# Four edits to a transformer kernel: table loads, mixers' softmax, token parts, the last expert pair

## The chip, the cores and the metric

The kernel runs on one core of one Trainium2 chip. A core has TensorE (PE, matmuls and transposes), VectorE (DVE), ScalarE (ACT), GpSimd (POOL) and SyncE (SP, which issues the DMAs here); they run at the same time and wait for one another by semaphores. Each engine takes its own instructions strictly in order. The metric is the device time of one execution in microseconds (us). One profiled execution supplies the trace.

## The reference

One sequence of 256 tokens, 1024 wide, all weights float32. Cut to what matters:

```python
for l in range(2):                                     # first block, two layers
    x = x + 0.5 * swiglu_ffn(rms_norm(x, g1[l]), ...)  # width 2816
    h = rms_norm(x, mix_norm[l]); proj = h @ w_in[l]
    y_ret = retention(...)                             # 4 heads of 128, rms_norm, * silu(gate)
    y_mla = mla_attention(...)                         # 8 heads of 64 + 32 rotary, causal
    x = x + concat([y_ret, y_mla]) @ w_o[l]
    x = x + 0.5 * swiglu_ffn(rms_norm(x, g2[l]), ...)
# second block: attention over 8 query and 2 key heads (both directions), a gated
# recurrence in both directions, then routing: the best 2 of 32 experts for each token
s = einsum('bhqd,bhkd->bhqk', qb, kf) * scale          # both attentions
p = softmax(s); o = einsum('bhqk,bhkd->bhqd', p, vf)
```

An expert keeps at most its capacity of tokens; a path for tokens beyond it stands behind a branch on their count.

## The kernel before

The kernel's stages follow one another: feed-forward 1 and mixer 1 and feed-forward 2 of layer 0, the same of layer 1, mixer 2, and the experts (`moe`).

In the dense stages a weight comes from HBM in 1-MB pieces (`loaded`, L319) into a ring of four buffers. `pieces` cuts each 128x1024 part into a high half `wh` on ACT (L332) and a remainder `wl` on DVE (L342). A product is the sum of high by high, high by low and low by high: L360 and L363 in the feed-forward, L284 to L286 in the mixers. L380 adds the bank sums of a feed-forward step, and L509 and L513 make the gated product. SP issues a load when its buffer is free.

`load_small` is a generator that the first feed-forward calls once per step from step HOOK_AT on. Its steps load the constant tables (L164), the gain columns (L175), the gain rows (L195), and the router weights (L203, L204). The last step also multiplies these by a gain on POOL (L207) and calls `rotary`, which loads the positions (L235) and works out sine and cosine tables on DVE.

In mixer 1, `mla` transposes queries and keys (`heads_T`, L612), and `scores` of a head pair computes score banks `s0` and `s1`, their maxima (L688, L689), the negative scaled maximum (L690), four exponentials on ACT (L693), reciprocals (L695), and the product with these, on DVE (L696) and on POOL (L697). PE then transposes the probabilities (L123, `pb`). The `retention` generator runs interleaved with it; its output `y` is multiplied by the gate on DVE (L807) and transposed.

In mixer 2, `attention` transposes queries and keys (`xa`; `kx` is the key pair with halves swapped, L899), copies them to `qT` (L897) and `kE` (L903, L904), and has one loop of nine turns: scores of (head pair, token half) in each of eight turns, and the transposes of the turn before. L916 to L923 are its softmax. The gated recurrence's work (L976 to L1112) and the big product interleave with it.

The order on each engine is the tile framework's: a scheduler with a simulated timeline sets it when the kernel is built, from the code's dependences, the interleaving of the generators, and the buffers of each tile.

In `moe`, L1329 and L1330 split the tokens into a rounded part `hk[0]` and a remainder `hk[1]`. L1381 to L1387 give each token its slot, L1495 and L1496 make the factors `gg` by which PE gathers tokens for four experts (L1508). Experts run in 16 pairs: gate and up (L1527), the hidden values (L1548), their transposes (L123), down (L1574) and the scatter back (L1599). Weights stream through 18 buffers of 1 MB; `blocks` sets the order of the loads, and the main loop at the end of `moe` sets that of the compute. The last pair's down weights come in smaller pieces (`LAST`).

Of the kernel before, what the change touches and what calls it, by code (L numbers as in the profile page):

```python
# [19 lines left out]
S = 256  # L20
DFF = 2816
EPS = 1e-6
P = 128
# [15 lines left out]
HOOK_AT = 3  # L39
# [58 lines left out]
def emit(ctx, tc, A, out):  # L98
# [61 lines left out]
    def load_small():  # L160
        cst = []
# [43 lines left out]
        late.update(cst=cst, gcol=gcol, rw=rw, gperm=gperm)  # L205

        nc.gpsimd.tensor_tensor(rw, rw, gains("g_ffn_2", 0)[:, :, None].to_broadcast([P, 8, 40]), op=ALU.mult)  # L207
        rotary()
# [25 lines left out]
    def rotary():  # L234
        nc.sync.dma_start(posi, A["positions"].rearrange("o (t p) -> p (o t)", p=P))  # L235
        with tc.tile_pool(name="rp", bufs=1) as rp:
# [315 lines left out]
    def mixer1(l):  # L552
        w_in, w_o = A["w_in"][l], A["w_o"][l]
        xp, rs = norm_parts(gains("mix_norm", 8 * l)), norm()
        with tc.tile_pool(name="mx", bufs=2) as m:
            yp = [None, pair_tile(m, [P, 4, S], "y1", bufs=1)]
            gtab = {}
            for nm in ("qn_rope", "kn_rope"):
# [7 lines left out]
                gtab[nm] = (tcos, tsin)  # L566
            cmask = m.tile([P, P], BF16, name="cmask", bufs=1)
# [39 lines left out]
            def heads_T(dst, src, t, gname):  # L607
                for h0 in (0, 4):
                    ps = aux_bank().rearrange("p (a t) -> p a t", a=4)
                    for h in range(4):  # L610
                        flip(ps[:96, h], src[:, h0 + h], ident)
                    nc.scalar.activation(dst[:96, h0:h0 + 4, t * P:(t + 1) * P], ps[:96], AF.Copy,  # L612
                                         scale=gains(gname, l, 1)[:96])

            def mla():
# [53 lines left out]
                scale = 96.0 ** -0.5  # L669
                po = None  # L670
                def scores(hp):
# [16 lines left out]
                    nc.vector.tensor_reduce(mx[:, 0:2], s0, axis=AX.X, op=ALU.max)  # L688
                    nc.vector.tensor_reduce(mx[:, 2:4], s1, axis=AX.X, op=ALU.max)  # L689
                    nc.vector.tensor_scalar(mx[:, 0:4], mx[:, 0:4], -scale, None, op0=ALU.mult)  # L690
                    for i, (dst, src) in enumerate(((p0[:, 0], s0[:, 0]), (p0[:, 1], s0[:, 1]), (p1[:, 0], s1[:, 0]),
                                                    (p1[:, 1], s1[:, 1]))):
                        nc.scalar.activation(dst, src, AF.Exp, bias=mx[:, i:i + 1], scale=scale,  # L693
                                             accum_out=mx[:, 4 + i:5 + i])
# [69 lines left out]
            def retention():  # L764
# [40 lines left out]
                for t in range(2):  # L805
                    y = ys[t]
                    nc.vector.tensor_tensor(y, rg[:, t], y, op=ALU.mult)  # L807
# [16 lines left out]
    def mixer2():  # L824
# [3 lines left out]
        with tc.tile_pool(name="m2l", bufs=1) as ml:  # L828
# [33 lines left out]
            def attention():  # L862
                for nm in ("q_norm_2", "k_norm_2"):
# [7 lines left out]
                    tab[nm] = (tcos, tsin)  # L871
                qT = late4("qT", [P, 4, S])
                kE = late4("kE", [P, 2, 2, S])
                nc.gpsimd.memset(kE, 0.0)
                for t in range(2):
# [21 lines left out]
                    nc.scalar.activation(qT[:, :, ts], ps, AF.Copy)  # L897
                    kx = m.tile([P, 2, 64], F32, tag="kx", name="kx", bufs=1)
                    nc.vector.tensor_copy(kx, x[:, 8:10][:, ::-1])  # L899
                    ps = aux_bank().rearrange("p (a t) -> p a t", a=4)  # L900
                    flip(ps[:, 0], x[:, 8:10].rearrange("p h d -> p (h d)"), ident)
                    flip(ps[:, 1], kx.rearrange("p h d -> p (h d)"), ident)
                    nc.vector.tensor_copy(kE[0:64, :, 0, ts], ps[0:64, 0:2])  # L903
                    nc.vector.tensor_copy(kE[64:128, :, 1, ts], ps[64:128, 0:2][:, ::-1])  # L904
                    yield
                asc = 64.0 ** -0.5
                po = None

                def scores(hp, t):
# [5 lines left out]
                    mx = m.tile([P, 4], F32, tag="mx", name="mx")  # L915
                    nc.vector.tensor_reduce(mx[:, 0:2], ps, axis=AX.X, op=ALU.max)  # L916
                    nc.vector.tensor_scalar(mx[:, 0:2], mx[:, 0:2], -asc, None, op0=ALU.mult)
                    pb = m.tile([P, 2, S], F32, tag="pb", name="pb")
                    for j in range(2):
                        nc.scalar.activation(pb[:, j], ps[:, j], AF.Exp, bias=mx[:, j:j + 1], scale=asc,  # L920
                                             accum_out=mx[:, 2 + j:3 + j])
# [819 lines left out]
```

## Time and profile before

| | |
|---|---|
| runs | 1708.24, 1712.7, 1713.85 us (median 1712.7) |
| profiled execution | 1712.65 us, span 1710.9 us, mean granted clock 0.99 |
| PE busy | 1647.1 us (96%) |
| DVE busy | 1004.8 us (59%) |
| ACT busy | 711.2 us (42%) |
| POOL busy | 361.4 us (21%) |
| DMA | 407.77 MB, mean 238 GB/s |

The first feed-forward fills the time to about 120 us, the mixers of layers 0 and 1 stand around 250 to 310 and 720 to 830 us, the second mixer's attention around 1045 to 1130, and the experts go from 1235 to the end. A share of busy time is a mean over stages with different limits: in the dense stages PE has the work, in the experts the weights' stream does. So waits and windows are to be read stage by stage. In a window's row the columns are busy microseconds, with the number of instructions in brackets; PEclk is TensorE's granted clock, as a share of the full 2.4 GHz, in which 0.5 is the lower level of 1.2 GHz.

### The profile page before, as it was taken

To read this page: it belongs to the slowest core of one execution; us is meant where nothing else is said; L and a number is where in the kernel's file an instruction comes from. 1 tells how busy PE (TensorE), PEld (TensorE's weight loads), DVE (VectorE), ACT (ScalarE), POOL (GpSimd) and SP (SyncE) were. 2 spreads that over 40 slices of the span, in tenths; PEclk is the share of its full clock that TensorE was granted. 3 is DMA by queue.
4 is the path that set the end of the run, shared out by engine and by line. 5 is a ranking of instruction groups with operands and counts; after the bars stand their busy time and mean duration, and the time that the engine had idled before them with its cause. 6 is when DMAs were issued, how large, how long until landed. Compare 5 with 4: busy or idle time off the path is not lost.

```text
span 1710.9 us, 23281 instructions
## 1 busy us (share of the span) xinstructions
PE 1647.1 (96%) x9169; PEld 1234.4 (72%) x9169; DVE 1004.8 (59%) x1571; ACT 711.2 (42%) x1097; POOL 361.4 (21%) x308
## 2 busy tenths in 40 slices
PE   8999998999999999999999999899899999999997
PEld 6788887888888888877888889789744444434332
DVE  6796687876667676787876668976742222211111
ACT  5554466465545554565555446644300000000001
POOL 6333322332222222311422230430400000000000
PEclk9999999999999999999999999999999999999999
DMA  9556552565556555533565565334979999999996
GB/s 315 168 176 200 163 172 75 170 186 186 180 190 195 177 188 174 174 124 122 174 190 174 184 195 168 124 100 150 418 293 404 420 419 421 419 420 421 419 421 263
DMA packets 216598, 407.77 MB, mean 238 GB/s; under 512 B 10063, under 2 KB 177190, under 8 KB 192166
## 3 DMA queue, kind: packets, MB, share of 16 engines
q1 hardware_dynamic: 216486, 406.25, 66.2%
q8 instruction: 74, 1.21, 0.3%
q14 instruction: 38, 0.31, 0.1%
HBM read 405.17 MB, written 1.05 MB: 237 GB/s over the span
## 4 chain that ended last, share of the span: by engine, by line
PE 76%; DMA 11%; DVE 6%; POOL 3%; issue 2%; ACT 1%; SPq 1%; POOLq 0%; DVEq 0%; ACTq 0%
PE mm L360 28%; PE mm L363 14%; PE aux L1527 8%; DMA raw<-in_w_exp_down_dram 6%; PE aux L1574 4%; PE mm L284 4%; PE mm L285 4%; PE mm L286 4%; DMA raw<-in_w_exp_gate_dram 2%; DMA raw<-in_w_exp_up_dram 2%; DVE wl L342 2%; PE aux L1508 2%; PE mm L1599 1%; PE aux L123 1%; ACT wh L332 1%
## 5 line engine op out<-in xcount | busy, mean ns | idle before, releaser
L342 DVE TENSOR_TENSOR wl<-raw,wh 128x1024 fp32r<-128x1024 f32 (+4 forms) x392 | 504.4, 1288 | 207.6 <-ACT wh L332 205.4
L332 ACT ACTIVATE wh<-raw 128x1024 fp32r<-128x1024 f32 (+3 forms) x392 | 405.7, 1037 | 364.0 <-PE mm L360 202.4
L360 PE MATMUL mm<-x,wh 128*128 128x512 f32 x1456 | 483.6, 398 | 10.6 <-DVE gu L380 5.3
L363 PE MATMUL mm<-x,wl 128*128 128x256 f32 x1456 | 361.8, 282 | 0.0
L360 PEld LDWEIGHTS mm<-x,wh 128*128 128x128 f32 x1456 | 271.4, 189 | 74.9 <-DVE gu L380 6.2
L363 PEld LDWEIGHTS mm<-x,wl 128*128 128x128 f32 x1456 | 256.2, 189 | 4.2
L1527 PE MATMUL aux<-raw,xg 128*64 128x512 f32 x1024 | 242.3, 598 | 7.8 <-DMA raw<-in_w_exp_up_dram 7.8
L360 PE MATMUL mm<-h,wh 128*128 128x512 f32 x704 | 246.6, 393 | 0.0
L509 POOL TENSOR_TENSOR gu<-gu,rb 128x512 f32<-128x512 f32 x88 | 141.9, 1616 | 322.9 <-DVE gu L380 299.8
L363 PE MATMUL mm<-h,wl 128*128 128x256 f32 x704 | 196.6, 279 | 0.0
L1527 PEld LDWEIGHTS aux<-raw,xg 128*64 128x64 f32 x1024 | 74.9, 137 | 148.4 <-issue 130.1
L360 PEld LDWEIGHTS mm<-h,wh 128*128 128x128 f32 x704 | 131.9, 187 | 31.6
L1574 PE MATMUL aux<-raw,hd 128*64 128x512 f32 x512 | 136.0, 597 | 4.6 <-DMA raw<-in_w_exp_down_dram 4.6
L363 PEld LDWEIGHTS mm<-h,wl 128*128 128x128 f32 x704 | 131.9, 187 | 0.0
L383 ACT ACTIVATE yp<-aux 128x512 fp32r<-128x512 f32 x32 | 19.1, 597 | 243.8 <-PE aux L1574 243.8
L1574 PEld LDWEIGHTS aux<-raw,hd 128*64 128x64 f32 x512 | 44.8, 136 | 84.2 <-issue 67.2
L1548 DVE SCALAR_TENSOR_TENSOR hid<-aux,cols,g 128x512 f32<-128x512 f32 x16 | 18.0, 1124 | 141.4 <-PE aux L1527 141.4
L384 DVE TENSOR_TENSOR yp<-aux,yp 128x512 fp32r<-128x512 f32 x32 | 22.1, 691 | 109.6 <-ACT yp L383 109.6
L285 PE MATMUL mm<-wl,x 128*128 128x512 f32 (+2 forms) x208 | 78.9, 382 | 0.8 <-DVE wl L342 0.8
L284 PE MATMUL mm<-wh,x 128*128 128x512 f32 (+2 forms) x208 | 77.1, 384 | 1.3 <-ACT wh L332 1.3
L286 PE MATMUL mm<-wh,x 128*128 128x512 f32 (+2 forms) x208 | 78.3, 380 | 0.0
L284 PE MATMUL mm<-x,wh 128*128 128x256 f32 x272 | 78.2, 287 | 0.0
(404 smaller groups left out, 2187.8 us busy)
## 6 DMA issues: line engine op xcount, KB each, us to landing
raw<-in_w_exp_gate_dram SPq DMA_DIRECT2D x64, 1024.0 KB
raw<-in_w_exp_up_dram SPq DMA_DIRECT2D x64, 1024.0 KB
raw<-in_w_exp_down_dram SPq DMA_DIRECT2D x62, 1024.0 KB
raw<-in_ffn_w_up_dram SPq DMA_DIRECT2D x44, 1024.0 KB
raw<-in_ffn_w_gate_dram SPq DMA_DIRECT2D x43, 1024.0 KB
raw<-in_w_in_dram SPq DMA_DIRECT2D x36, 1024.0 KB
raw<-in_ffn_w_down_dram SPq DMA_DIRECT2D x32, 1024.0 KB
raw<-in_ffn_w_down_dram SPq DMA_DIRECT2D x16, 768.0 KB
```

What stands on the lines that cost most here:

```text
L284: nc.tensor.matmul(ps, a[0], b[0], start=first, stop=False, skip_group_check=True)
L285: nc.tensor.matmul(ps, a[0], b[1], start=False, stop=False, skip_group_check=True)
L286: nc.tensor.matmul(ps, a[1], b[0], start=False, stop=last, skip_group_check=True)
L332: nc.scalar.activation(h, r[:, k0:k1], AF.Copy)
L342: eng.tensor_tensor(lf, rf, hf.bitcast(F32), op=ALU.subtract)
L360: nc.tensor.matmul(banks[j], lhs, chunk_both(xp, kk), start=kk == 0, stop=False, skip_group_check=True)
L363: nc.tensor.matmul(banks[j][:, :S], lhs, chunk(xp, kk)[0], start=False, stop=kk == k_all - 1, skip_group_check=True)
L384: nc.vector.tensor_tensor(dst[1][sl], src, dst[0][sl].bitcast(F32), op=ALU.subtract)
L509: nc.gpsimd.tensor_tensor(e, e, twice(rb), op=ALU.mult)
L1508: nc.tensor.matmul(ps[:, i], src[:, t, (k0 + i) * P:(k0 + i + 1) * P], gs[t][:, q0:q0 + n], start=(i, j, t) == terms[0], stop=(i, j, t) == ...
L1527: nc.tensor.matmul(ps[half(s)], xg[:, k, at + s * SLOT:at + (s + 1) * SLOT], w[s][:, k % 4], start=k == 0, stop=k == 7, skip_group_check=True)
L1574: nc.tensor.matmul(pss[hf][half(s)], hd[:, ff, half(s)], w[s][:, ff - ks.start, hf * 512 - c0:(hf + 1) * 512 - c0], start=ff == 0, stop=ff ...
```

## The change

Four edits.

1. The hook starts at step 2 of the first feed-forward in place of 3. The positions are loaded first in it. `rotary` is a generator now: its work is spread over three more steps.
2. In mixer 1 the score factor goes into the query gain column (`gqs`), the reduces return the negated maximum, and L690 is gone. The gate products of both halves of `y` stand ahead of a yield.
3. In mixer 2 the factor goes into the copy `qT`, L917 is gone likewise, `kx` and `kE` are copied by ACT, and the probabilities are transposed two turns behind their scores, with three buffers of `mx` and `pb`.
4. In `moe` the remainder `hk[1]` is taken on DVE, and for the last pair the down weights of the pair before are loaded, and multiplied, ahead of its own up weights.

```diff
-HOOK_AT = 3
+HOOK_AT = 2
@@ load_small
+        nc.sync.dma_start(posi, A["positions"].rearrange("o (t p) -> p (o t)", p=P))
         cst = []
...
         late.update(cst=cst, gcol=gcol, rw=rw, gperm=gperm)
+        yield
         nc.gpsimd.tensor_tensor(rw, rw, gains("g_ffn_2", 0)[:, :, None].to_broadcast([P, 8, 40]), op=ALU.mult)
-        rotary()
+        yield from rotary()
@@ rotary
-        nc.sync.dma_start(posi, A["positions"].rearrange("o (t p) -> p (o t)", p=P))
...
             nc.vector.scalar_tensor_tensor(n1, nh, -4096.0, n1, op0=ALU.mult, op1=ALU.add)
+            yield
             for c in parts:
...
             for i, (shift, add) in enumerate(((0.25, math.pi / 2), (0.0, 0.0))):
+                yield
                 whole(n1, ang, 1 / (2 * math.pi), shift)
@@ mixer1
+            gcols = {"qn_nope": m.tile([P, 1], F32, name="gqs", bufs=1), "kn_nope": gains("kn_nope", l, 1)}
+            nc.vector.tensor_scalar(gcols["qn_nope"], gains("qn_nope", l, 1), 96.0 ** -0.5, None, op0=ALU.mult)
...
-                                         scale=gains(gname, l, 1)[:96])
+                                         scale=gcols[gname][:96])
...
-                    nc.vector.tensor_reduce(mx[:, 0:2], s0, axis=AX.X, op=ALU.max)
-                    nc.vector.tensor_reduce(mx[:, 2:4], s1, axis=AX.X, op=ALU.max)
-                    nc.vector.tensor_scalar(mx[:, 0:4], mx[:, 0:4], -scale, None, op0=ALU.mult)
+                    nc.vector.tensor_reduce(mx[:, 0:2], s0, axis=AX.X, op=ALU.max, negate=True)
+                    nc.vector.tensor_reduce(mx[:, 2:4], s1, axis=AX.X, op=ALU.max, negate=True)
...
-                        nc.scalar.activation(dst, src, AF.Exp, bias=mx[:, i:i + 1], scale=scale,
-                                             accum_out=mx[:, 4 + i:5 + i])
+                        nc.scalar.activation(dst, src, AF.Exp, bias=mx[:, i:i + 1], accum_out=mx[:, 4 + i:5 + i])
...
                 for t in range(2):
+                    nc.vector.tensor_tensor(ys[t], rg[:, t], ys[t], op=ALU.mult)
+                yield
+                for t in range(2):
                     y = ys[t]
-                    nc.vector.tensor_tensor(y, rg[:, t], y, op=ALU.mult)
@@ mixer2
-                    nc.scalar.activation(qT[:, :, ts], ps, AF.Copy)
-                    kx = m.tile([P, 2, 64], F32, tag="kx", name="kx", bufs=1)
-                    nc.vector.tensor_copy(kx, x[:, 8:10][:, ::-1])
+                    nc.scalar.activation(qT[:, :, ts], ps, AF.Copy, scale=asc)
+                    kx = m.tile([P, 2 * S], F32, tag="osq", name="kx", bufs=1)[:, :P]
+                    nc.scalar.activation(kx.rearrange("p (h d) -> p h d", h=2), x[:, 8:10][:, ::-1], AF.Copy)
...
-                    nc.vector.tensor_copy(kE[0:64, :, 0, ts], ps[0:64, 0:2])
-                    nc.vector.tensor_copy(kE[64:128, :, 1, ts], ps[64:128, 0:2][:, ::-1])
+                    nc.scalar.activation(kE[0:64, :, 0, ts], ps[0:64, 0:2], AF.Copy)
+                    nc.scalar.activation(kE[64:128, :, 1, ts], ps[64:128, 0:2][:, ::-1], AF.Copy)
...
-                    mx = m.tile([P, 4], F32, tag="mx", name="mx")
-                    nc.vector.tensor_reduce(mx[:, 0:2], ps, axis=AX.X, op=ALU.max)
-                    nc.vector.tensor_scalar(mx[:, 0:2], mx[:, 0:2], -asc, None, op0=ALU.mult)
-                    pb = m.tile([P, 2, S], F32, tag="pb", name="pb")
+                    mx = m.tile([P, 4], F32, tag="mx", name="mx", bufs=3)
+                    nc.vector.tensor_reduce(mx[:, 0:2], ps, axis=AX.X, op=ALU.max, negate=True)
+                    pb = m.tile([P, 2, S], F32, tag="pb", name="pb", bufs=3)
...
-                pT, last = None, None
-                for i in range(9):
+                pT, pbs = None, []
+                for i in range(10):
                     if i < 8:
-                        pb = scores(i // 2, i % 2)
-                    if last is not None:
-                        hp, t = (i - 1) // 2, (i - 1) % 2
+                        pbs.append(scores(i // 2, i % 2))
+                    if i > 1:
+                        last = pbs[i - 2]
+                        hp, t = (i - 2) // 2, (i - 2) % 2
@@ moe
-                    nc.gpsimd.tensor_tensor(hk[1][:, t], xs[:, t], hk[0][:, t].bitcast(F32), op=ALU.subtract)
+                    nc.vector.tensor_tensor(hk[1][:, t], xs[:, t], hk[0][:, t].bitcast(F32), op=ALU.subtract)
...
+                            if w is wg_ and p == NP - 1:
+                                yield from downs(p - 1)
...
-                    elif p:
-                        for fh in range(2):
-                            for e in (2 * p - 2, 2 * p - 1):
-                                yield by_rows(wd_[e], 4)[:, 2 * fh:2 * fh + 2], 2
+                    elif 0 < p < NP - 1:
+                        yield from downs(p - 1)
...
+                if p == NP - 1:
+                    ys[p - 1] = down(p - 1)
                 if p < NP:
                     run(up(p))
                     run(coming)
-                if p:
+                if p and p != NP - 1:
                     ys[p - 1] = down(p - 1)
```

`downs(p)` yields the four 1-MB down pieces of a pair. Lines of the changed file stand 1 to 11 further down than the same lines before.

What this does to the order. SP in the first feed-forward, where the hook's loads stand among the weights; before, the last of them:

```order
L195 DMA brow_846<-in_b_router_expert_dram 128x32
L319 DMA raw<-in_ffn_w_gate_dram 128x8x256
L319 DMA raw<-in_ffn_w_up_dram 128x8x256
L202 DMA gperm<-in_g_ffn_dram 128x8
L203 DMA rw<-in_w_router_group_dram 128x8x4
L204 DMA rw<-in_w_router_expert_dram 128x8x32
L235 DMA posi<-in_positions_dram 128x2x1
L319 DMA raw<-in_ffn_w_gate_dram 128x8x256
L319 DMA raw<-in_ffn_w_up_dram 128x8x256
```

and now, the first of them:

```order
L322 DMA raw<-in_ffn_w_gate_dram 128x8x256
L322 DMA raw<-in_ffn_w_up_dram 128x8x256
L161 DMA posi<-in_positions_dram 128x2x1
L165 DMA cst_510<-in_cst_dram 128x1744
L165 DMA cst_512<-in_cst_dram 128x1536
L165 DMA cst_514<-in_cst_dram 128x448
L322 DMA raw<-in_ffn_w_gate_dram 128x8x256
L322 DMA raw<-in_ffn_w_up_dram 128x8x256
```

The positions come before the constant tables, and both ahead of the fourth pair of weight loads instead of the fifth; the three router loads (L203 to L205 now) keep their order and stand one pair of weights earlier too.

PE in the second mixer, from the first scores (`kE,qT`) to the second transposes of probabilities (`pb`); the rows left out are L284 to L286 of the big product. Before:

```order
L913 MATMUL aux<-kE,qT 128x256 x4
L284 MATMUL mm<-x_9399,wh 128x256
...
L286 MATMUL mm<-x_9399,wl 128x256
L123 MATMUL aux<-ident,pb 128x128 x4
L1074 MATMUL aux<-qp,kp 128x128 x8
L913 MATMUL aux<-kE,qT 128x256 x2
L123 MATMUL aux<-ident,pb 128x128 x4
L1074 MATMUL aux<-qp,kb 128x128 x8
L945 MATMUL mm<-pT,xa 64x256 x4
```

and now:

```order
L287 MATMUL mm<-x_9394,wh 128x256
L918 MATMUL aux<-kE,qT 128x256 x2
L288 MATMUL mm<-x_9394,wh 128x256
...
L918 MATMUL aux<-kE,qT 128x256 x2
L1078 MATMUL aux<-qp,kp 128x128 x8
L287 MATMUL mm<-x_9395,wh 128x256
...
L289 MATMUL mm<-x_9395,wl 128x256
L918 MATMUL aux<-kE,qT 128x256 x2
L287 MATMUL mm<-x_9394,wh 128x256
...
L288 MATMUL mm<-x_9394,wh 128x256
L123 MATMUL aux<-ident,pb 128x128 x4
L1078 MATMUL aux<-qp,kb 128x128 x8
L289 MATMUL mm<-x_9394,wl 128x256
```

Three sets of scores and the product `qp,kp` stand ahead of the first transposes, where two sets stood, and 43 rows lie between the first scores and these transposes in place of 21.

DVE at the same place, with the softmax (reduce, reciprocal, product) among weight remainders. Before:

```order
L342 TENSOR_TENSOR wl<-raw,wh 128x1024
L976 SCALAR_TENSOR_TENSOR hgs<-th,hgs 128x512
L916 TENSOR_REDUCE mx<-aux 128x2 x2
L1026 TENSOR_SCALAR hgs<-hgs,gcol 128x512
L917 TENSOR_SCALAR mx<-mx 128x2 x2
L1024 TENSOR_TENSOR hgs<-mm,rb 128x512
L342 TENSOR_TENSOR wl<-raw,wh 128x1024
L922 RECIPROCAL mx<-mx 128x2
L923 TENSOR_TENSOR pb<-pb,mx 128x512
L922 RECIPROCAL mx<-mx 128x2
L923 TENSOR_TENSOR pb<-pb,mx 128x512
```

and now:

```order
L345 TENSOR_TENSOR wl<-raw,wh 128x1024
L921 TENSOR_REDUCE mx<-aux 128x2 x2
L345 TENSOR_TENSOR wl<-raw,wh 128x1024
L1081 COPY_PREDICATED A<-cst_512,aux 128x4x128
L926 RECIPROCAL mx<-mx 128x2
L1081 COPY_PREDICATED A<-cst_512,aux 128x4x128
L926 RECIPROCAL mx<-mx 128x2
L927 TENSOR_TENSOR pb<-pb,mx 128x512 x2
L1028 TENSOR_TENSOR hgs<-mm,rb 128x512
L921 TENSOR_REDUCE mx<-aux 128x2
L345 TENSOR_TENSOR wl<-raw,wh 128x1024
```

The scaling of the maximum is gone, one weight remainder and two masked copies of `A` stand between the reduces and the products, and `hgs` is worked on later.

PE at the end of the program, the last two pairs of experts. Before:

```order
L1599 MATMUL mm<-yp,gt 128x512 x2
L1527 MATMUL aux<-raw,xg 64x512 x31
L1574 MATMUL aux<-raw,hd 64x512 x2
L123 MATMUL aux<-ident,hid 128x128 x4
L1574 MATMUL aux<-raw,hd 64x512 x14
L1599 MATMUL mm<-yp,gt 128x512 x6
L1574 MATMUL aux<-raw,hd 64x512 x2
L1599 MATMUL mm<-yp,gt 128x512 x2
L1574 MATMUL aux<-raw,hd 64x512 x13
L1599 MATMUL mm<-yp,gt 128x512 x2
L1574 MATMUL aux<-raw,hd 64x512
L1599 MATMUL mm<-yp,gt 128x512 x6
```

and now:

```order
L1608 MATMUL mm<-yp,gt 128x512 x2
L1536 MATMUL aux<-raw,xg 64x512 x15
L1583 MATMUL aux<-raw,hd 64x512 x16
L1608 MATMUL mm<-yp,gt 128x512 x6
L1536 MATMUL aux<-raw,xg 64x512
L1608 MATMUL mm<-yp,gt 128x512 x2
L1536 MATMUL aux<-raw,xg 64x512 x15
L123 MATMUL aux<-ident,hid 128x128 x4
L1583 MATMUL aux<-raw,hd 64x512 x16
L1608 MATMUL mm<-yp,gt 128x512 x8
```

Sixteen rows of down (`raw,hd`) of pair 14 and its scatter stand ahead of the last up, and all sixteen of pair 15 stand in one piece ahead of the last eight of the scatter.

## Rows read from the trace of the kernel before

**Rows 1.** The page: the chain of waits by engine; GB/s in 40 slices
```profile
PE 76%; DMA 11%; DVE 6%; POOL 3%; issue 2%; ACT 1%; SPq 1%; POOLq 0%; DVEq 0%; ACTq 0%
GB/s 315 168 176 200 163 172 75 170 186 186 180 190 195 177 188 174 174 124 122 174 190 174 184 195 168 124 100 150 418 293 404 420 419 421 419 420 421 419 421 263
```
**Rows 2.** Waits of PE: line, releaser, total us, times, longest
```profile
PE aux L1527 <- DMA raw<-in_w_exp_up_dram: 7.8, 8, 1.3
PE aux L1508 <- DVE gg L1496: 6.3, 1, 6.3
PE aux L123 <- DVE mx L922: 6.1, 2, 4.4
...
PE aux L123 <- DVE pb L696: 1.8, 1, 1.8
PE aux L123 <- DVE y L807: 1.5, 1, 1.5
PE aux L123 <- DVE kx L899: 1.5, 1, 1.5
```
**Rows 3.** Windows: us, busy PE, PEld, DVE, ACT, POOL, PEclk, DMA share, GB/s
```profile
80.00:85.00 5.00, 5.00 (x17) 4.26 (x16) 5.00 (x9) 1.86 (x4) 1.11 (x1) 0.52 0.65 210
...
290.00:295.00 5.00, 2.48 (x17) 1.88 (x18) 4.86 (x8) 2.68 (x8) 1.19 (x1) 0.80 0.35 110
295.00:300.00 5.00, 5.00 (x20) 4.04 (x20) 2.09 (x5) 1.24 (x3) 0.00 (x0) 0.52 0.00 0
...
785.00:790.00 5.00, 5.00 (x28) 3.54 (x28) 4.22 (x8) 2.99 (x6) 1.21 (x1) 0.71 0.00 0
...
1095.00:1100.00 5.00, 5.00 (x29) 4.78 (x28) 3.25 (x7) 1.88 (x3) 0.00 (x0) 0.66 0.60 201
...
1240.00:1245.00 5.00, 1.35 (x6) 1.38 (x7) 4.24 (x8) 0.00 (x0) 2.48 (x2) 0.50 1.00 415
1245.00:1250.00 5.00, 5.00 (x21) 2.93 (x20) 0.85 (x2) 0.00 (x0) 0.00 (x0) 0.63 0.06 26
```
**Rows 4.** Timeline at 76 to 80: start, us, engine, line, instruction, idle before
```profile
76.62 0.17 DVE L238 CAST pos<-posi 128x2 f32<-128x2 int32 x1 [5.62 <-DMA posi<-in_positions_dram]
...
79.49 3.78 PE L360 MATMUL mm<-x,wh 128*128 128x512 f32 x8 [3.78 <-DVE gu L380]
```
**Rows 5.** Timeline of DVE and ACT in mixer 1 of layer 1
```profile
775.67 0.42 DVE L688 TENSOR_REDUCE mx<-aux 128x2 f32<-128x256 f32 x1 [0.21 <-PE aux L681]
...
779.04 1.28 ACT L693 ACT_TABLE_LOAD   x1 [3.15 <-DVE mx L690]
```
**Rows 6.** Timeline of DVE in mixer 2
```profile
1089.90 1.28 DVE L916 TENSOR_REDUCE mx<-aux 128x2 f32<-128x512 f32 x2
```
**Rows 7.** Timeline of POOL and DVE in the routing; the page's group of L342
```profile
1237.84 4.64 POOL L1330 TENSOR_TENSOR hk<-xs,hk 128x1024 fp32r<-128x1024 f32 x2 [4.91 <-ACT hk L1329]
...
1238.06 2.15 DVE L1381 TENSOR_SCALAR over<-rank 128x4 f32<-128x4 f32 x1
1240.12 0.15 DVE L1382 SCALAR_TENSOR_TENSOR slot<-idx,rank 128x4 f32<-128x4 uint32 x1
1240.31 2.19 DVE L1383 SCALAR_TENSOR_TENSOR slot<-over,slot 128x4 f32<-128x4 f32 x1
...
1257.98 0.29 DVE L1416 TENSOR_SCALAR at<-cst,rank 128x128 f32<-128x128 f32 x1 [1.07 <-PE aux L1420]
...
L342 DVE TENSOR_TENSOR wl<-raw,wh 128x1024 fp32r<-128x1024 f32 (+4 forms) x392 | 504.4, 1288 | 207.6 <-ACT wh L332 205.4
```
**Rows 8.** Timeline of PE and DVE in the last two pairs
```profile
1674.99 3.22 PE L1527 MATMUL aux<-raw,xg 128*64 128x512 f32 x13 [1.32 <-DMA raw<-in_w_exp_up_dram]
...
1678.75 1.09 DVE L1548 SCALAR_TENSOR_TENSOR hid<-aux,cols,g 128x512 f32<-128x512 f32 x1 [15.81 <-PE aux L1527]
...
1692.67 6.22 PE L1574 MATMUL aux<-raw,hd 128*64 128x512 f32 x26
...
1703.12 0.73 PE L1599 MATMUL mm<-yp,gt 128*128 128x512 f32 x2 [0.39 <-DVE yp L384]
```

More of the change, by code (lines that the diff above doesn't have):

```diff
@@ L667, in mla @@
                     yield
-                scale = 96.0 ** -0.5
                 po = None
@@ L871, in attention @@
                     tab[nm] = (tcos, tsin)
+                asc = 64.0 ** -0.5
                 qT = late4("qT", [P, 4, S])
@@ L896, in attention @@
                         flip(ps[:, a], x[:, 2 * a:2 * a + 2].rearrange("p h d -> p (h d)"), ident)
-                    nc.scalar.activation(qT[:, :, ts], ps, AF.Copy)
-                    kx = m.tile([P, 2, 64], F32, tag="kx", name="kx", bufs=1)
-                    nc.vector.tensor_copy(kx, x[:, 8:10][:, ::-1])
+                    nc.scalar.activation(qT[:, :, ts], ps, AF.Copy, scale=asc)
+                    kx = m.tile([P, 2 * S], F32, tag="osq", name="kx", bufs=1)[:, :P]
+                    nc.scalar.activation(kx.rearrange("p (h d) -> p h d", h=2), x[:, 8:10][:, ::-1], AF.Copy)
                     ps = aux_bank().rearrange("p (a t) -> p a t", a=4)
                     flip(ps[:, 0], x[:, 8:10].rearrange("p h d -> p (h d)"), ident)
-                    flip(ps[:, 1], kx.rearrange("p h d -> p (h d)"), ident)
-                    nc.vector.tensor_copy(kE[0:64, :, 0, ts], ps[0:64, 0:2])
-                    nc.vector.tensor_copy(kE[64:128, :, 1, ts], ps[64:128, 0:2][:, ::-1])
+                    flip(ps[:, 1], kx, ident)
+                    nc.scalar.activation(kE[0:64, :, 0, ts], ps[0:64, 0:2], AF.Copy)
+                    nc.scalar.activation(kE[64:128, :, 1, ts], ps[64:128, 0:2][:, ::-1], AF.Copy)
                     yield
-                asc = 64.0 ** -0.5
                 po = None
@@ L914, in scores @@
                                          skip_group_check=True)
-                    mx = m.tile([P, 4], F32, tag="mx", name="mx")
-                    nc.vector.tensor_reduce(mx[:, 0:2], ps, axis=AX.X, op=ALU.max)
-                    nc.vector.tensor_scalar(mx[:, 0:2], mx[:, 0:2], -asc, None, op0=ALU.mult)
-                    pb = m.tile([P, 2, S], F32, tag="pb", name="pb")
+                    mx = m.tile([P, 4], F32, tag="mx", name="mx", bufs=3)
+                    nc.vector.tensor_reduce(mx[:, 0:2], ps, axis=AX.X, op=ALU.max, negate=True)
+                    pb = m.tile([P, 2, S], F32, tag="pb", name="pb", bufs=3)
                     for j in range(2):
-                        nc.scalar.activation(pb[:, j], ps[:, j], AF.Exp, bias=mx[:, j:j + 1], scale=asc,
+                        nc.scalar.activation(pb[:, j], ps[:, j], AF.Exp, bias=mx[:, j:j + 1],
                                              accum_out=mx[:, 2 + j:3 + j])
@@ L949, in attention @@
                                 split(ap_, (slice(None), slice(hp - 1, hp + 1)), po)
-                    last = pb if i < 8 else None
                     yield
@@ L1447, in blocks, with downs @@
             def blocks():
+                def downs(p):
+                    for fh in range(2):
+                        for e in (2 * p, 2 * p + 1):
+                            yield by_rows(wd_[e], 4)[:, 2 * fh:2 * fh + 2], 2
                 for p in range(NP + 1):
```

## The prediction

> **What bounds the kernel now.** The chain of waits comes first: it runs through TensorE (PE) for 76% of the span and through DMA for 11% [rows 1]. So a saving on another engine counts only where PE stands still or is throttled. The table of PE's waits is read next. Its long single entries are the ones that the change touches: 6.3 us for the gather factors L1496, 4.4 us in one piece for the softmax sums L922 of the second mixer, and 1.5 to 1.8 us each for L696, L807 and L899 [rows 2]. The largest entry of all, the experts' up weights, is 1.3 us at the most in one piece and is not touched. Then the windows: the reader is to look for a small PE busy time and, in the same or the next window, a granted clock under 1.00 [rows 3]. A stall is paid twice here. PE idles, and what follows runs at half its level (0.52 is nearly all at 1.2 GHz). I count the second part as PE's busy time in the window times one minus its clock. Last, the rate of DMA over the span: from the experts' first loads on it stays at 418 to 421 GB/s, with a dip to 293 [rows 1] that holds the window 1245:1250 (26 GB/s) [rows 3], where loads wait for buffers that PE has not read yet. So the experts' stream resumes when PE resumes, and I pass every microsecond won before it on to the end.
>
> **Small loads and rotary tables.** The cast of the positions stands on VectorE (DVE) behind their DMA, which SP issues behind the router weights; DVE idles 5.62 us for it, and L380, queued behind it, comes late: PE waits 3.78 us [rows 4]. The window 80:85 has PE full at 0.52, so 2.4 us more: 6.2 us in all [rows 3]. In the new order the positions load first of all in the hook, and the table is spread over three more steps. That wait must go. What can come late in its place is L380 behind one weight remainder (L342, 1.29 us, rows 7) and some table operations, since the same DVE work has to go somewhere. I take 4.5, with 0 and 6.2 as ends. The price on SP: positions and three constant tables (1.9 MB) now stand one weight pair earlier. I cost this at nothing because those weights have a PE step ahead of them; without that cover it is the fourth rival.
>
> **First mixer, twice.** Scale and sign go into the queries and the reduce, so each head pair loses L690, and its first exponentials wait for the first reduce alone. In layer 1 that reduce starts at 775.67 and lasts 0.42, but the exponentials' table load starts at 779.04, released by L690 [rows 5]. It can now start at about 776.1, 2.9 us earlier; the second pair of exponentials still needs L689. PE's 1.8 us wait for L696 [rows 2] and the 1.4 us at clock 0.71 [rows 3] come to 3.2. I take 3, ends 0 and 4.5 (a wait for POOL's half of the probabilities goes too, unseen in these rows). In layer 0 the products L807 of both halves stand one yield earlier, so their 1.5 us goes [rows 2]; windows 290:295 and 295:300 hold 2.52 idle and 2.4 lost to the clock [rows 3], 4.9 in all. PE also waits there for copies that do not change, so I take 2, ends 0 and 4.9.
>
> **Second mixer.** Scores of a head pair are now two steps ahead of their transposes: a third copy of two tiles. DVE loses eight 128x2 instructions at about 0.15 (nearest: L1382, rows 7), two key copies and four half-height copies. ScalarE gains the six copies; it is busy for 1.88 of 5 us in the window 1095:1100 [rows 3], so there is room, but not in a certain place. What PE waits 4.4 us for is a reduce that starts at 1089.90 [rows 6] because DVE is full, then exponentials and a product. In the new order 43 rows of PE lie between the first scores and their transposes in place of 21, and on DVE one weight remainder and two masked copies between reduce and product. PE idle 4.4 and 1.5, with 1.7 lost at 0.66 [rows 2, 3] plus the second wait for L922 (6.1 less 4.4 is 1.7): 9.3 if all goes. DVE carries the same weight work in the same stretch, so two thirds can come back as other waits, and moving PE's instructions ahead can add one wait as long as the one removed. Ends -3 and 9.3; I take 3, nearer to the waits whose cause is removed outright (1.5 and 1.7) than to the sum.
>
> **Routing.** POOL's two subtractions L1330 take 4.64 us. Beside them DVE's L1381 takes 2.15 and L1383 2.19, while L1382, of the same 128x4, takes 0.15 [rows 7]. They are the path to L1496, for which PE waits 6.3. With the subtractions on DVE, which orders them behind the gather factors, 4.0 us goes. They cost DVE two times 1.29 (L342, two inputs, same size), ahead of the combine weights that L1420 multiplies; DVE stands idle for 1.07 us there, waiting for PE [rows 7], so 1.5 of the 2.6 is late: 2.5. If the shorter gap also spares the clock (0.50 and 0.63 in two windows, 0.7 and 1.9 us, rows 3), 5.1. Ends -1.5 and 5.1, I take 2.5. The Trainium skill, page "SBUF — State Buffer", section "Who interferes with whom", says that a VectorE instruction with two SBUF inputs, or in its two-port mode, and a GpSimd instruction share one port pair, and the later of them is blocked for the whole of the other. By that rule the 4.0 are POOL's and go; without it only the coincidence of these rows speaks for it, the term would be -1.5, and the sum 4.0 less. It also says that the moved subtractions could block or be blocked by POOL in their new place; POOL is at 0.00 in the window 1245:1250 [rows 3], so the trace of before shows it nothing to meet there.
>
> **Last pair.** Down of pair 14 goes ahead of up of pair 15. Up's second half now waits for 4 MB more: 1674.99 [rows 8] plus 10.0 at 419 GB/s, 1685.0. The path from there to down 15 is hid (3.76 us after it, 1.09 long, rows 8), transposes and a copy, 6.3 in all: 1691.3. Then 32 matmuls at 0.24 (26 in 6.22) end at 1698.9, and the last scatter starts 1.8 later, as before, or when the other scatters queued behind are through, at 1701.2 against 1703.12 [rows 8]. I take 2, ends -1 and 3.
>
> **Sum.** 4.5 + 3 + 2 + 3 + 2.5 + 2 = 17.0 us off the profiled execution's own 1712.65 us (span 1710.9, the rest around it), which equals the median of the runs, 1712.7. That gives 1696.
>
> **Rivals.**
> 1. Waits move. DVE stays the engine that PE waits for, and only the two waits go that have an outside cause: the positions' DMA (3.78) and POOL's neighbours (2.5): 1706. For it: DVE is above 4 of 5 us busy in four of the seven windows of rows 3. Against: four of six terms shorten chains, not only loads.
> 2. The experts' stream hides routing and last pair: 4.5 less, 1700. For it: 419 GB/s to the end. Against: 26 GB/s in 1245:1250.
> 3. All the ends at once, the clock held too: 6.2 + 4.5 + 4.9 + 6 + 5.1 + 2 = 29, 1684. Against: full DVE windows.
> 4. Slower: ScalarE becomes late in the second mixer. It takes the six copies and, with scores at other places among the gates, its function tables may be switched back and forth around the exponentials, 1.28 us a load [rows 5], 2.6 a switch and return. Over eight steps that is 20.5 us on the path. With the other terms won (14.0) it ends at 1719, and it decides from six switched steps on. Against: the exponentials stand among the gates without loads now. The hook's loads are the smaller case of this kind: 4.6 us of transfer (1.9 MB at 419 GB/s), not enough alone.
> 5. It does not relieve what it moves: the order's new places make other waits as long, 1712.
>
> **How the numbers follow.** My forecast 0.47, rival 1 0.22, rival 2 0.08, rival 3 0.08, rival 4 0.07, rival 5 0.08. About 0.3%, 5 us, can be told from no change, so faster means under 1707.6. Rival 1 falls there in three of four cases: faster 0.47 + 0.08 + 0.08 + 0.16 = 0.79; same 0.06 + 0.08 = 0.14; slower 0.07. The forecast's own range is 1690 to 1702 (a third of the terms' spread each way). The range for 8 in 10 reaches from 1686 to 1709: it takes in rivals 1 and 2 and leaves out 3, 4 and 5.
>
> **What would show it.** Right: no idle time of DVE behind the positions, and no window under 1.00 at 75 to 85; the exponentials' table load of layer 1 right behind L688; L1381 and L1383 (L1385 and L1387 after) at 0.2; the wait for L1496 at some 2 us; the second mixer's wait for L922 under 2; scatter last at about 1.9 us sooner against up's arrival. Wrong: DVE waits of the same length under another name in the same windows (rival 1), table loads between the exponentials of the second mixer and PE waiting for ScalarE (rival 4), or a span of the experts that grows by what the dense part loses (rival 2).

## The result

The changed kernel takes 1694.5 us (median of 4 runs, 1692.9 to 1695.7), the kernel before 1712.1 in the runs beside it. The ratio is 0.9900 with a 95% interval of 0.9884 to 0.9916, that is 14 to 20 us less. Forecast were 1696, and 17.0 less. The sum held; its terms did not, as the stages show.

The page after: the chain by engine, and the rate of DMA, as in [rows 1].

```profile
PE 69%; DMA 19%; DVE 6%; ACT 2%; issue 2%; POOL 1%; SPq 0%; ACTq 0%; DVEq 0%; POOLq 0%
GB/s 294 199 174 200 169 164 85 150 198 177 185 188 190 183 184 182 179 140 86 199 186 188 181 193 176 125 124 147 420 321 405 420 420 420 420 421 420 420 421 294
```

PE's waits after (line, releaser, total, times, longest). Of those in [rows 2], L922 and L899 are gone, and L1505 (L1496 before) is at 2.5 for 6.3. New are many short waits for L383 (L380 before) and one of 2.8 for y.

```profile
PE mm L363 <- DVE gu L383: 5.9, 6, 1.5
...
PE aux L123 <- DVE y L809: 3.1, 2, 2.8
...
PE aux L1517 <- DVE gg L1505: 2.5, 2, 2.3
...
PE aux L123 <- DVE pb L699: 1.1, 1, 1.1
```

To place the time, I take the start of the same PE instruction in both timelines at each stage's border (the norm's L430 ahead of the next stage, L1137, L1370, the first L1574, the end of the last scatter L1599; L360's end for the first feed-forward). What its lead over the kernel before grows by within a stage is that stage's gain. The table has it for the changed kernel's trace, and for those of the five kernels below that hold one edit alone; positive is gained, in us; bold is the stage that the edit changes. The stretches between these stages are left out.

| stage | forecast | after | hook_alone | mix1_alone | mix2_alone | hk_alone | last_alone |
|---|---|---|---|---|---|---|---|
| first feed-forward (32 to 205) | 4.5 | 1.0 | **2.0** | -0.3 | 0.3 | 0.1 | 0.0 |
| mixer 1, layer 0 (214 to 338) | 2 | -1.0 | 0.2 | **-2.7** | 2.8 | 2.8 | 1.1 |
| mixer 1, layer 1 (710 to 834) | 3 | 4.1 | 0.7 | **4.2** | 0.8 | 0.0 | -1.2 |
| mixer 2 (1020 to 1154) | 3 | 9.3 | -1.5 | -0.5 | **9.3** | -0.5 | -0.6 |
| routing (1237 to 1290) | 2.5 | 3.5 | -0.2 | -0.1 | 0.2 | **3.0** | 0.3 |
| experts (1290 to the last scatter) | 2 | 2.9 | 0.0 | -0.5 | 0.2 | -0.1 | **1.2** |

The columns show also what one execution can move without any edit: 0.2 to 2.8 us in layer 0's mixer, whose code is the same in four of the five, and 1.8 the other way in layer0_old below.

### The profile page after: what moved, and what is told of

It is laid out like the page before. It is cut to its first block, busy times and chain, and to the rows that moved or that the text cites. A ratio compares the mean times of both kernels' runs of the same rounds, so it can differ in the third digit from the quotient of the medians.

```text
span 1691.1 us, 23257 instructions
## 1 busy us (share of the span) xinstructions
PE 1637.6 (97%) x9169; PEld 1230.0 (73%) x9169; DVE 997.1 (59%) x1553; ACT 712.6 (42%) x1103; POOL 359.2 (21%) x306
## 4 chain that ended last, share of the span: by engine, by line
PE 69%; DMA 19%; DVE 6%; ACT 2%; issue 2%; POOL 1%; SPq 0%; ACTq 0%; DVEq 0%; POOLq 0%
PE mm L363 29%; PE mm L366 15%; DMA raw<-in_w_exp_down_dram 8%; DMA raw<-in_w_exp_gate_dram 6%; DMA raw<-in_w_exp_up_dram 5%; PE mm L287 4%; PE mm L288 4%; PE mm L289 4%; PE aux L1536 4%; DVE wl L345 2%; PE aux L1583 2%; PE aux L123 1%; PE aux L1517 1%; ACT wh L335 1%; PE mm L1608 1%
## 5 line engine op out<-in xcount | busy, mean ns | idle before, releaser
L335 ACT ACTIVATE wh<-raw 128x1024 fp32r<-128x1024 f32 (+3 forms) x392 | 405.2, 1036 | 364.6 <-PE mm L363 199.3
L512 POOL TENSOR_TENSOR gu<-gu,rb 128x512 f32<-128x512 f32 x88 | 142.3, 1620 | 321.6 <-DVE gu L383 298.6
L287 PE MATMUL mm<-wh,x 128*128 128x512 f32 (+2 forms) x208 | 77.2, 384 | 1.3 <-ACT wh L335 1.3
L382 ACT ACTIVATE gu<-mm 128x256 f32<-128x256 f32 x176 | 63.4, 374 | 34.9 <-PE mm L366 34.9
```

The costliest lines, as they stand in the source:

```text
L287: nc.tensor.matmul(ps, a[0], b[0], start=first, stop=False, skip_group_check=True)
L335: nc.scalar.activation(h, r[:, k0:k1], AF.Copy)
L382: nc.scalar.activation(dst[:, j], b[:, S:], AF.Copy)
L512: nc.gpsimd.tensor_tensor(e, e, twice(rb), op=ALU.mult)
```

## The experiments

All are timed in 5 rounds beside the kernel before. The first five hold one edit each, on the kernel before (hk_alone and last_alone hold half of edit 4 each).

**hook_alone**, edit 1 alone. 

> The kernel before with edit 1 alone (hook from step 2, positions first, tables spread over steps). Theory A, the parts are worth what the shift of PE between the stages of the two traces says: 1.0 us faster than before; DVE never waits for the positions, PE waits for L380 some five times for 0.3 to 1.4 us between 65 and 115, no window there under clock 1.00. Theory B, the forecast's term: 4.5 us faster, at most one such wait. Theory C, the parts depend on one another: neither.

Measured: 1708.3 us, ratio 0.9986 (0.9973 to 0.9998), 0.3 to 4.6 us less. Theory A's 1.0 lies inside that, the term of 4.5 at its edge. In its own trace the waits for L380's counterpart are five, 3.4 us in all, and the stage gains 2.0. Its window from 65 to 115 (columns as in rows 3):

```profile
65.00:115.00 50.00, 46.64 (x260) 39.77 (x259) 45.63 (x86) 25.14 (x42) 15.34 (x10) 1.00 0.62 191
```

The same window, and one from 255 to 305 that is read further down, of the kernel before:

```profile
65.00:115.00 50.00, 46.22 (x251) 40.23 (x250) 42.74 (x82) 23.99 (x41) 15.79 (x9) 0.93 0.63 194
255.00:305.00 50.00, 44.95 (x263) 37.00 (x262) 37.39 (x64) 30.10 (x66) 10.56 (x9) 0.93 0.23 72
```

and of the changed kernel:

```profile
255.00:305.00 50.00, 43.73 (x259) 35.02 (x258) 34.92 (x58) 29.68 (x67) 10.62 (x9) 0.93 0.20 64
65.00:115.00 50.00, 45.65 (x256) 39.04 (x255) 44.59 (x85) 25.08 (x42) 16.28 (x10) 1.00 0.60 190
```

In the first feed-forward PE is idle for 3.78 us before [rows 4], 3.36 in hook_alone and 4.35 in the changed kernel. So what the edit won there is the clock (0.93 to 1.00), and next to nothing of the idle time. Counted from 32 by the start of the same matmuls, the changed kernel's lead is 4.2 us at 85 and 0.7 at 118: the old stall goes, and the new waits give most of it back.

**mix1_alone**, edit 2 alone. 

> The kernel before with edit 2 alone (first mixer). Theory A: 2.8 us faster, as 1.1 lost in layer 0 (one wait of 2.8 us for L807's y and half a clock behind it) and 3.9 won in layer 1. Theory B: 5 us faster, 2 of them in layer 0. Theory C: the loss in layer 0 comes from what the other edits did before it and is not there.

Measured: 1708.3 us, 0.9980 (0.9969 to 0.9992), 1.4 to 5.3 less. Theory A by its parts: layer 0 loses (2.7, more than in the changed kernel), layer 1 wins 4.2. So the loss in layer 0 comes with this edit alone; theory C falls.

**mix2_alone**, edit 3 alone. 

> The kernel before with edit 3 alone (second mixer). Theory A: 9.3 us faster, no wait over 1.3 us of PE and no clock under 1.00 in the second mixer's attention. Theory B: 3 us faster, with waits of PE for other DVE results in the place of those removed.

Measured: 1700.1 us, 0.9932 (0.9917 to 0.9946), 9.2 to 14.2 less. Theory A: 9.3 in the trace, and these two waits are all that PE has from 1035 to 1155, where the kernel before had 9.0 us of them:

```profile
PE aux L1111 <- POOL ks L1104: 1.2, 1, 1.2
PE aux L123 <- DVE pb L922: 0.4, 1, 0.4
```

**hk_alone**, the token remainder on DVE alone.

```diff
-                    nc.gpsimd.tensor_tensor(hk[1][:, t], xs[:, t], hk[0][:, t].bitcast(F32), op=ALU.subtract)
+                    nc.vector.tensor_tensor(hk[1][:, t], xs[:, t], hk[0][:, t].bitcast(F32), op=ALU.subtract)
```

> The kernel before with the token remainder on DVE alone. Theory A: 3.5 us faster, L1381 and L1383 at 0.2 us each and the wait for L1496 at 2.3 us. Theory B: 2.5 us. If the two instructions stay at 2.1 us without POOL beside them, POOL was not their cause.

Measured: 1707.9 us, 0.9980 (0.9967 to 0.9993), 1.2 to 5.6 less. PE's wait for the gather factors falls by 4.0 (6.3 to 2.3); 3.0 of that are left when the combine weights have come late by 0.9. The timeline of DVE, to be laid beside [rows 7]:

```profile
1234.09 0.17 DVE L1381 TENSOR_SCALAR over<-rank 128x4 f32<-128x4 f32 x1
1234.16 0.15 DVE L1382 SCALAR_TENSOR_TENSOR slot<-idx,rank 128x4 f32<-128x4 uint32 x1
1234.35 0.16 DVE L1383 SCALAR_TENSOR_TENSOR slot<-over,slot 128x4 f32<-128x4 f32 x1
```

The same kernel has something that I did not look for. Its windows in the unchanged mixer of layer 0:

```profile
290.00:295.00 5.00, 2.61 (x23) 1.95 (x22) 4.68 (x8) 2.80 (x7) 1.19 (x1) 1.00 0.31 105
295.00:300.00 5.00, 5.00 (x33) 4.32 (x32) 3.07 (x7) 3.21 (x10) 0.96 (x1) 1.00 0.00 0
```

PE is idle as long as in the same windows of [rows 3] (2.39 and 2.52 us), but the clock stays at 1.00 where it had been 0.80 and 0.52. That is the 2.8 us of the table: after a stall of this length the lower clock came in one execution and not in another.

**last_alone**, the order of the last pair alone. 

> The kernel before with the order of the last pair alone. Theory A, from the shift between 1613 and the last scatter in the two traces: 2.9 us faster. Theory B, the forecast's term by rows: 2 us. Rival: the loads hide it, 0.

Measured: 1711.3 us, 0.9993 (0.9981 to 1.0004): from 3.3 less to 0.7 more, not told from none; 1.2 in its trace, 2.9 in the changed kernel's.

**nohoist**, the changed kernel with the products of y in their old place.

```diff
-                for t in range(2):
-                    nc.vector.tensor_tensor(ys[t], rg[:, t], ys[t], op=ALU.mult)
-                yield
                 for t in range(2):
                     y = ys[t]
+                    nc.vector.tensor_tensor(y, rg[:, t], y, op=ALU.mult)
```

> The changed kernel with the gate products of y back in their old place (each ahead of its own transposes). Theory D: the hoist makes the first transposes of y in layer 0 wait for more of DVE; without it PE's idle time from 255 to 305 falls by 1.2 us or more, and the kernel is 1 to 2 us faster than the changed one. Rival: the softmax edits made that wait, and the idle time stays within 0.3 us.

Measured: 1693.9 us, 0.9892 (0.9873 to 0.9911), not to be told from the changed kernel. Its window, and its timeline of PE, in layer 0:

```profile
255.00:305.00 50.00, 44.41 (x261) 36.06 (x259) 36.27 (x62) 29.88 (x67) 10.61 (x9) 0.93 0.21 65
```

```profile
291.20 1.09 PE L123 MATMUL aux<-ident,y 128*128 128x128 f32 x4 [2.74 <-ACT th L764]
294.39 1.09 PE L123 MATMUL aux<-ident,y 128*128 128x128 f32 x4 [0.62 <-DVE y L810]
```

Idle time falls by 0.68 us (44.41 less 43.73), under the 1.2 of theory D and over the rival's 0.3. The long wait stays and has another releaser, the gate's activation L764. The whole loss of idle time in layer 0 is 1.22 us (44.95 before, 43.73 after). So the early products of y make 0.68 of it, and 0.54 are left, with the long wait. What makes these can be read on ScalarE. There the first exponentials wait for L693 alone now, ScalarE is idle 2.82 us for it, and all four of a head pair stand ahead of the gate's first `th`. ScalarE in the changed kernel:

```profile
285.53 0.37 ACT L697 ACTIVATE pb<-aux,mx 128x128 f32<-128x128 f32 x1 [2.82 <-DVE mx L693]
...
287.25 0.49 ACT L697 ACTIVATE pb<-aux,mx 128x256 f32<-128x256 f32 x1
...
287.69 0.65 ACT L764 ACTIVATE th<-rg 128x512 f32<-128x512 f32 x1
...
290.21 0.66 ACT L764 ACTIVATE th<-rg 128x512 f32<-128x512 f32 x1
```

and in the kernel before, where the gate's first half stood ahead of them:

```profile
284.57 0.63 ACT L761 ACTIVATE th<-rg 128x512 f32<-128x512 f32 x1
...
288.88 0.37 ACT L693 ACTIVATE pb<-aux,mx 128x128 f32<-128x128 f32 x1
```

This is theory G of layer0_old. That order is read from the timelines; no run moved it alone.

**mix2_lag1**, one step between scores and transposes again.

```diff
-                for i in range(10):
+                for i in range(9):
...
-                    if i > 1:
-                        last = pbs[i - 2]
-                        hp, t = (i - 2) // 2, (i - 2) % 2
+                    if i > 0:
+                        last = pbs[i - 1]
+                        hp, t = (i - 1) // 2, (i - 1) % 2
```

> The changed kernel with the second mixer's probabilities transposed one step behind their scores again; three buffers, folded factor and ScalarE's copies stay. Theory E, the second step is what hides the softmax chain: 4 to 6 us slower than the changed kernel, with a wait for L922's counterpart of some 2 to 4 us. Rival F, DVE's relief is what pays: under 1.5 us slower.

Measured: 1702.2 us, 0.9936 (0.9920 to 0.9953): 7.7 us above the changed kernel's median, 6.2 by the ratios to the kernel before. The mixer's own gain falls from 9.3 to 2.4. Theory E in direction, with more than its 4 to 6; but not with its wait, since PE waits for another engine:

```profile
PE aux L1116 <- POOL ks L1109: 5.4, 1, 5.4
PE aux L123 <- DVE pb L927: 0.9, 1, 0.9
```

**mix2_dve**, the copies on VectorE again, the two steps kept.

```diff
-                    nc.scalar.activation(kx.rearrange("p (h d) -> p h d", h=2), x[:, 8:10][:, ::-1], AF.Copy)
+                    nc.vector.tensor_copy(kx.rearrange("p (h d) -> p h d", h=2), x[:, 8:10][:, ::-1])
...
-                    nc.scalar.activation(kE[0:64, :, 0, ts], ps[0:64, 0:2], AF.Copy)
-                    nc.scalar.activation(kE[64:128, :, 1, ts], ps[64:128, 0:2][:, ::-1], AF.Copy)
+                    nc.vector.tensor_copy(kE[0:64, :, 0, ts], ps[0:64, 0:2])
+                    nc.vector.tensor_copy(kE[64:128, :, 1, ts], ps[64:128, 0:2][:, ::-1])
```

> The changed kernel with the copies kx and kE on VectorE again, the two-step order kept. Theory E: 0 to 2 us slower, the 1.5 us wait for kx comes back. Rival F: 4 us or more slower, since DVE is full there.

Measured: 1699.7 us, 0.9924 (0.9906 to 0.9941): 5.2 above the changed kernel's median, 4.1 by the ratios, whose intervals overlap a little (this one begins at 0.9906, the changed kernel's ends at 0.9916). That is rival F, at its lower end; the trace says it more plainly, since the mixer's gain falls from 9.3 to 2.5, with waits under new names:

```profile
PE aux L123 <- ACT pb L924: 3.1, 1, 3.1
PE aux L918 <- ACT pb L924: 1.0, 1, 1.0
PE aux L123 <- DVE kx L905: 0.5, 1, 0.5
```

So neither half alone carries the edit: each without the other is worth 2.4 or 2.5, both 9.3. The folded factor and the third buffers are in all three, and what they would do without either half was not run.

**layer0_old**, edit 2 in layer 1 only: the old softmax and the old place of L807 for `l == 0`, the new ones for `l == 1`. 

> The changed kernel with the first mixer's edit in layer 1 only; layer 0 as before. Theory G: in layer 0 the earlier exponentials stand ahead of the gate's activations on ScalarE, which make y late, so the edit loses there; without it the stage from 214 to 338 takes 2 to 3 us less on the mean (idle 2.9 in place of 4.1, and the clock as it falls), the whole 1 to 3 us less than the changed kernel. Rival: the loss is one execution's clock, and nothing changes beyond 0.5 us.

Measured: 1691.3 us, 0.9885 (0.9868 to 0.9902). The interval reaches into that of the changed kernel. Its window 255:305 has PE at 44.95, and so do those of the kernel before and of all that leave layer 0 alone; 43.67 to 43.75 is what the whole edit makes of it (mix1_alone too). So edit 2 is shown to cost 1.22 us of idle time in layer 0; that the order on ScalarE does it, as theory G says, is shown by no run, and 0.68 of it went with the early products in nohoist. In this execution the stage took 1.8 us more than in the trace of before, with a lower clock (0.90 for 0.93), so theory G's 2 to 3 us was not met in it. On the mean of all executions it is: the six kernels with the whole edit lose 0.9 to 2.9 in this stage (1.9 on the mean), the seven with the old layer 0 stand between 1.8 lost and 2.8 won (1.1 won).

**nospread**, the tables in one step. 

> The changed kernel with the rotary tables in one step (step 6 of the first feed-forward) in place of four; positions first and hook from step 2 as changed. Theory I, the tables' DVE time is paid anyway: within 1 us of the changed kernel, waits for L380's counterpart of the same sum (4.4 us) at other places. Rival: the spreading is what makes the five short waits; without it they go, 2 to 4 us faster. Second rival: one long wait with half a clock, 2 us or more slower.

Measured: 1692.9 us, 0.9901 (0.9885 to 0.9918). Theory I: the same five waits, 4.25 us for 4.35, so the spreading does not make them. What goes on at the third of them, in the changed kernel, POOL first, then DVE, ScalarE, DVE and PE:

```profile
83.43 3.19 POOL L512 TENSOR_TENSOR gu<-gu,rb 128x512 f32<-128x512 f32 x1 [4.27 <-DVE gu L383]
...
85.24 0.23 DVE L253 TENSOR_SCALAR n<-ang 128x160 f32<-128x160 f32 x1
85.50 1.22 DVE L254 TENSOR_SCALAR n<-n 128x160 f32<-128x160 f32 x1
86.76 0.24 DVE L255 TENSOR_SCALAR n<-n 128x160 f32<-128x160 f32 x1
...
86.65 0.63 ACT L515 ACTIVATE gu<-gu 128x512 f32<-128x512 f32 x1 [3.96 <-POOL gu L512]
87.19 1.04 ACT L335 ACTIVATE wh<-raw 128x1024 fp32r<-128x1024 f32 x1
...
88.26 1.22 DVE L345 TENSOR_TENSOR wl<-raw,wh 128x1024 fp32r<-128x1024 f32 x1 [0.90 <-ACT wh L335]
...
90.11 2.10 PE L363 MATMUL mm<-x,wh 128*128 128x512 f32 x8 [1.21 <-DVE gu L383]
```

L254 is as large as its neighbours, and takes 1.0 us longer, until POOL is done; one table operation in most steps is held like that. But this is not what PE waits for here: DVE stands idle for 0.90 us after it, until ScalarE has the next high half (L335), which is queued behind L515, and that behind POOL's L512, which takes 3.19 us here and 1.31 in the steps before and after. The kernel before holds its table operations just so, and PE is busy all the time beside them:

```profile
87.85 1.29 DVE L262 SCALAR_TENSOR_TENSOR ang<-nh,ang 128x160 f32<-128x160 f32 x1
...
91.81 1.31 DVE L262 SCALAR_TENSOR_TENSOR ang<-nh,ang 128x160 f32<-128x160 f32 x1
```

```profile
85.00:115.00 30.00, 30.00 (x172) 26.19 (x171) 29.69 (x57) 15.99 (x28) 9.85 (x5) 1.00 0.57 176
```

So why the five waits come is open; no run took POOL out of these steps.

**pool_late**, the remainder on GpSimd again, held back by a one-column result that DVE makes after the gather factors.

```diff
+                one = m.tile([P, 1], F32, name="one", bufs=1)
+                nc.vector.tensor_scalar(one, gg[:, 0:1], 0.0, 1.0, op0=ALU.mult, op1=ALU.add)
...
-                    nc.scalar.activation(hk[0][:, t], xs[:, t], AF.Copy)
-                    nc.vector.tensor_tensor(hk[1][:, t], xs[:, t], hk[0][:, t].bitcast(F32), op=ALU.subtract)
+                    nc.scalar.activation(hk[0][:, t], xs[:, t], AF.Copy, scale=one)
+                    nc.gpsimd.tensor_tensor(hk[1][:, t], xs[:, t], hk[0][:, t].bitcast(F32), op=ALU.subtract)
```

> The changed kernel with the token remainder on GpSimd again, but held back by a small DVE result until the gather factors are made. Theory H, the blocked port: the two 128x4 instructions stay at 0.2 us though POOL works 4.6 us as before; PE's wait of 0.9 us for the combine weights goes, 0 to 1 us faster than the changed kernel. Rival: another cause makes the 128x4 instructions long whenever POOL has this work: they take 2 us again, or others of DVE do.

Measured: 1688.2 us, 0.9871 (0.9852 to 0.9891), 6.3 below the changed kernel's median, 5.0 by the ratios, whose intervals just overlap (this one ends at 0.9891, the changed kernel's begins at 0.9884). Theory H for the routing:

```profile
1229.46 4.67 POOL L1336 TENSOR_TENSOR hk<-xs,hk 128x1024 fp32r<-128x1024 f32 x2 [9.00 <-ACT hk L1335]
...
1225.60 0.17 DVE L1387 TENSOR_SCALAR over<-rank 128x4 f32<-128x4 f32 x1
1225.68 0.15 DVE L1388 SCALAR_TENSOR_TENSOR slot<-idx,rank 128x4 f32<-128x4 uint32 x1
1225.87 0.16 DVE L1389 SCALAR_TENSOR_TENSOR slot<-over,slot 128x4 f32<-128x4 f32 x1
```

POOL works as long as in [rows 7], but behind the two DVE instructions, which are not held; PE's wait of 0.9 for the combine weights is gone, and the stage gains 4.4 (3.5 in the changed kernel). But 8.1 us more come after 1290, where the weights arrive faster; hence the last run.

**both_new**, layer0_old and pool_late in one. 

> The changed kernel with the first mixer's edit in layer 1 only and the token remainder on GpSimd behind the gather factors (the edits of layer0_old and pool_late together). In pool_late the experts' weights came at 427 GB/s for 420 in all other runs, which is 7 us of its 430 us stream. Theory J, that rate belongs to one loaded program and not to the edit: the rate is 420 here, the kernel 3 to 4 us faster than the changed one (1690 to 1691). Rival, the edit (its added tile moves the buffers behind it) makes the rate: 427 again, 1684 to 1686.

Measured: 1685.1 us, 0.9843 (0.9829 to 0.9857), faster than the changed kernel (whose interval begins at 0.9884). A window of the stream in it, then the same of the changed kernel:

```profile
1300.00:1350.00 50.00, 50.00 (x242) 22.02 (x238) 9.48 (x16) 4.12 (x7) 0.00 (x0) 1.00 1.01 427
1300.00:1350.00 50.00, 50.00 (x248) 22.40 (x246) 10.87 (x18) 4.78 (x8) 0.00 (x0) 1.00 1.01 420
```

427 GB/s again, and 419 to 421 from the 32nd of the page's 40 slices to the last but one in all twelve kernels without pool_late's edit (the changed one's stand above). Two of these, layer0_old and nospread, ran on the same chip as pool_late. Theory J falls. The rate comes with the edit; whether by the added tile, which may move the buffers behind it, or by something else in it, was not tried.

## Why the prediction was right, and where not

- **Small loads: mis-sized, 4.5 against 1.0 in the trace and 2.4 timed alone.** The wait for the positions went, as said. The step that failed is what could come late in its place, one weight remainder. It was five waits of 0.3 to 1.4 us for the same L380, 4.35 in all; at the one looked into, the remainder stood behind ScalarE and POOL, which the term did not have, and why all five come is open. What was won is the half clock, less 0.6 us of added idle time: 1.8 by the prediction's 2.4, 1.0 by the stage, and the difference is not accounted for. The nine kernels with edit 1 gain 1.0 to 2.0 here.
- **First mixer, layer 1: right, 3 against 4.1.** The exponentials' table load starts 3.3 earlier than in [rows 5], behind the scaling no more, and no window from 775 to 805 is under clock 1.00:

```profile
775.70 1.28 ACT L697 ACT_TABLE_LOAD   x1
```

- **First mixer, layer 0: wrong in sign, 2 against -1.0 and -2.7, of which the clock of one execution is a part; 1.22 us more of idle time are sure.** The step took from the wait for y what the edit removes. It did not ask what the earlier products put off (0.68 of the 1.22), nor what the earlier exponentials pass on ScalarE: the gate, which makes y (read from the timelines). The wait for y came back as 2.8, and 1.1 came for the probabilities.
- **Second mixer: right in mechanism, mis-sized, 3 against 9.3.** I kept a third of the 9.3 because DVE carries the same work in that stretch. It does: it is busy for 98.0 of 110 us after (1031 to 1141) and 102.0 of 120 before (1035 to 1155). But two steps of lag let its lateness pass without PE seeing it, once the six copies were off it as well. Rival 4 did not happen: PE waits nowhere there for ScalarE, and ScalarE loads its tables four times from 1020 to 1155, as before.
- **Routing: right, 2.5 against 3.5.** 4.0 at the gather; the combine weights cost 0.9 where 1.5 was reckoned. The Trainium skill's rule on the shared port pair (page "SBUF — State Buffer", section "Who interferes with whom"), without which the term would have been -1.5, agrees with hk_alone and pool_late: 0.16 us for 2.19 once the two don't meet.
- **Last pair: the size of 2 fits the 1.2 and 2.9 of the traces (timed alone it is not told from none), its path does not.** Up's second half was to wait for its load until 1685.0. PE in the changed kernel runs up without a wait for DMA, since down of pair 14 keeps it busy until the load has landed, and waits for the hidden values instead:

```profile
1665.15 7.08 PE L1536 MATMUL aux<-raw,xg 128*64 128x512 f32 x30
1673.41 0.66 PE L123 MATMUL aux<-ident,hid 128*128 128x128 f32 x4 [1.18 <-DVE hid L1557]
1674.82 7.14 PE L1583 MATMUL aux<-raw,hd 128*64 128x512 f32 x32 [0.75 <-ACT hd L1566]
1681.88 2.30 PE L1608 MATMUL mm<-yp,gt 128*128 128x512 f32 x8
```

- **The clock as a fixed price: wrong.** I put it into most stalls. After the stall of 3.8 us in the first feed-forward the clock of 65 to 115 fell in the kernel before (0.93) and in all four that keep the stall (0.97); after 2.4 us in layer 0's mixer it fell or not.

So the sum is right by luck, by two errors of opposite sign: 4.5 + 2 was 6.5 too much for 0, and the second mixer 6.3 too little. The chance of 0.79 for faster had its ground in the six separate places, and four of them gained. Rival 3 was added up wrong: it says all the ends at once, but takes 6 for the second mixer and 2 for the last pair, whose ends were 9.3 and 3; that sum is 33.0, and 1680.

## What to carry to other kernels

Before pricing a stall that an earlier result is to remove, list on each in-order engine what the earlier result now passes: what stood ahead of it is late in its turn. On a full engine, price lag and relief together, since each without the other gave a quarter of the gain here. Compare idle time by windows of the same stage first and the clock second: in layer 0's window idle time repeated to a hundredth over seven kernels with the same code there, and the clock ran from 0.90 to 1.00.

## What the hardware showed

- Some 2.4 us of idle time of PE left the granted clock at 1.00 (hk_alone) or took it to 0.52 (before), 2.8 us apart in the stage.
- Small DVE operations took 1.0 to 2.0 us longer while a POOL instruction ran: 0.24 to 1.22 (L254), 0.17 to 2.15 (L1381).
- With pool_late's edit (a 128x1 tile with its two uses, and the remainder on GpSimd) the stream of weights came at 427 GB/s for 420, on two chips: 1.6%, some 7 us of it. The cause is open.
